# Gate and up projection: five weight pairs by seven products in eight chunks, two subtractions per chunk on GpSimd, results turned one chunk later

## The chip, the core and the metric

The kernel runs on one core of one Trainium2 chip. The time is the device time of one execution in microseconds. The trace gives the work of TensorE (PE, with its weight loads as PEld), VectorE (DVE), ScalarE (ACT), GpSimd (POOL) and SyncE (SP, which here only issues DMAs). TensorE multiplies, VectorE and ScalarE prepare the weights and finish results, GpSimd adds while it transfers (accumulating DMAs).

## The reference, cut to what matters

Two layers over 256 tokens of width 2048, all in float32:

```python
for l in range(DEPTH):                      # 2
    h = rms_norm(x, pre_mix_norm[l])
    m = hybrid_mixer(h, l, w_in[l], w_o[l], ...)      # two kinds of attention
    x = x + rms_norm(m, post_mix_norm[l])
    h = rms_norm(x, pre_ffn_norm[l])
    f = (silu(h @ w_gate[l]) * (h @ w_up[l])) @ w_down[l]   # inner width 5632
    x = x + rms_norm(f, post_ffn_norm[l])
```

The change is in the gate and up projection, `h @ w_gate` and `h @ w_up`, and in what was done ahead of time for it in the output projection of the mixer.

## The kernel before

**Precision.** A float32 weight tile is split in two parts that TensorE multiplies at full rate: `hi`, the rounded value (ScalarE, L351), and `lo`, the rest, `raw - hi` (VectorE, L354; called a rest below). The activations are split in the same way, once. A product of float32 quality is three matmuls of 512 columns (`product`, L1113): high by `hi`, high by `lo`, low by `hi`.

**Chunks and pairs.** The inner width 5632 is cut into 11 chunks of 512 columns, c = 0 to 10. The sum over 2048 inputs is cut into 8 pairs `kp` of twice 128 rows. A weight tile is 128 x 1024: two K blocks of one pair and chunk. Per chunk, four PSUM banks hold gate and up for two groups of 128 tokens.

**Eight or seven.** A pair done plainly (`eight`) takes 2 K blocks x 2 token groups x 2 matrices = 8 products, 24 matmuls. Some pairs (`seven`, `seven_products`) use a scheme of seven products (21 matmuls) that treats gate and up of one pair as a 2 x 2 block matrix. It needs sums of weight tiles: T, the up tile with the gate tile's first half added by an accumulating DMA on GpSimd's queue (L298); then on VectorE the second half of T (L334), and G, the gate tile plus that (L335); each sum is split into high and low like a weight (L319 on ScalarE, L320 on VectorE: `hi`/`lo` of T, `Th`/`Tl` of the half and of G). It also needs sums of activations, made once per layer and pair by `pair_sums`, at places in the table `FORM_AT` of (chunk, place in the chunk): pair. Four more banks collect p1, p6, p7 and q5; at the end of the last seven of a chunk, `shared_part` (L1157 on ScalarE, L1158 to L1161 on VectorE) folds them into four tiles `w`, which are added to the chunk's four banks when these are done.

Which pairs go by seven is given by `gate_sevens` (L70): c=0 has two, c=1 three, most chunks four (pairs 2, 4, 5, 6), and the chunks in `MORE_AT`, 7 and 9, five (2 to 6). For these two chunks the sums of pairs 3 and 5 are made ahead of time by `foresee` (L244), while the output projection runs, stored to DRAM, and loaded back in `summed` (L281) as T, a third tile and W.

**Results.** At the end of a chunk VectorE adds `w` to the banks (L1308, L1310), ScalarE takes Silu (L1309), VectorE multiplies (L1311). `flip` then turns the result with four transposes per token group on TensorE (L1317) and a copy on ScalarE (L1318); it starts 7 ticks after the chunk's end, so in the middle of the next chunk's first pairs, each group at a tick of its own.

**Order.** The code calls engines in program order; a scheduler of the framework places instructions of different engines, and each engine, and each DMA queue, then works through its own list in order. The weights come in one stream in the order of use (`weight_order`, L77), with `LOOKAHEAD` four tiles split ahead. Buffers: `raw` 4, `hi` and `lo` 6 each, G 3, T 4. `not_ahead`, `behind` and `after_rests` keep some loads and VectorE instructions behind named others; `put_away` stores parts of x at the chunks in `AWAY_AT`.

Of the kernel before, what the change touches and what calls it, by code (L numbers as in the profile page):

```python
# [9 lines left out]
F32 = mybir.dt.float32  # L10
# [48 lines left out]
AWAY_AT = (3, 4, 5, 6)  # L59
# [6 lines left out]

FORESEEN_PER_LAYER = [(c, kp) for c in FORESEEN for kp in FORESEEN[c]]


def gate_sevens(c):  # L70

    if c in MORE_AT:
        return MORE_SEVEN
    return (FIRST_SEVEN, NEXT_SEVEN)[c] if c < 2 else SEVEN


def weight_order():  # L77
# [9 lines left out]
    for l in range(L):  # L87
# [14 lines left out]
        for c in range(FF // CW):  # L102
            for kp in FIRST_ORDER if c == 0 else range(KT // 2):
# [60 lines left out]
def kernel(  # L164
# [37 lines left out]

    ready = {}
# [3 lines left out]
    def fetch(upto):  # L207
        while len(raws) < min(upto, len(stream)):
            i = len(raws)
            for j in range(i, min(i + EARLY + 1, mix_raw[3])):  # L210
                if j in sevens and j not in sums and not (j in foreseen and j > i + 1):
# [30 lines left out]
    foreseen, found, thirds = {}, {}, []  # L242

    def foresee(l):  # L244

        jobs = [plan[l]["up"][c, kp] for c, kp in FORESEEN_PER_LAYER]
        tiles = {}

        def summed_up(i):
            g, u = tiles[i]  # L250
            k = kept.tile([P, 4, CW], F32, name=f"foreseen{i}")
            with after_rests():
                sums_in_place(g, u, True)
            nc.gpsimd.dma_start(k[:, 0:2, :], u)
            nc.gpsimd.dma_start(k[:, 2:4, :], g)
            foreseen[i] = k

        for n, i in enumerate(jobs):
            tiles[i] = [x_pool[0].tile([P, 2, CW], F32, tag="W", bufs=2 * len(jobs), name=f"{q}{i}") for q in ("Gf", "Tf")]
            for t, j in zip(tiles[i], (i - 1, i)):  # L260
                with in_turn():
                    nc.sync.dma_start(t, stream[j])
                yield AHEAD_PACE
            if n:
                summed_up(jobs[n - 1])
            yield AHEAD_PACE
        yield AHEAD_PACE
        summed_up(jobs[-1])

    def sums_in_place(g, u, first):  # L270

        t2 = u[:, 1, :]
        if first:
            nc.vector.tensor_tensor(out=u[:, 0, :], in0=g[:, 0, :], in1=u[:, 0, :], op=ALU.add)
        nc.vector.tensor_tensor(out=t2, in0=t2, in1=u[:, 0, :], op=ALU.subtract)
        nc.vector.tensor_tensor(out=g, in0=g, in1=t2.unsqueeze(1).to_broadcast([P, 2, CW]), op=ALU.add)

    def summed(i):

        if i in foreseen:  # L280
            kept_sums = foreseen[i]  # L281
            n = len(found)
            if n % len(FORESEEN_PER_LAYER) == 0:
                thirds.append(late_room([P, 2, CW], f"second{i}"))
            second = thirds[-1][:, n % 2, :]
            two = [mix_raw[0].tile([P, 2, CW], F32, tag="T", bufs=mix_raw[2], name=f"{q}{i}") for q in ("T", "W")]
            with not_ahead(i):
# [1196 lines left out]
```

## Time and profile before

| | |
|---|---|
| time, median of 3 runs | 2189.97 us (2189.87 to 2190.26) |
| span of the profiled execution | 2189.2 us |
| TensorE busy | 2174.7 us, 99% of the span |
| VectorE busy | 1921.7 us, 88% |
| ScalarE busy | 1378.0 us, 63% |
| GpSimd busy | 144.2 us, 7% |
| DMA | 489.30 MB, 224 GB/s on the mean |

The profile page gives the busy time of each engine, the chain of work that ended last, and groups of like instructions with their mean duration. Windows give the busy time of each engine in a stretch of the span, with the number of instructions; the timeline gives single instructions with start and duration. A matmul's row shows its length in the pipeline; what it costs is the distance between two starts. The gate and up projection of the first layer lies between about 397 and 862 us, that of the second between about 1486 and 1951 us.

### The profile page before, as it was taken

The page shows a single profiled execution, that of the slowest core. Times are in us where ns is not written, and L with a number is a line of the kernel's source. Part 1 is how long each engine was busy: PE and PEld are TensorE (multiplying, and loading weights), DVE is VectorE, ACT ScalarE, POOL GpSimd, SP SyncE. Part 2 cuts the span into 40 slices and gives each one's busy share as a digit, 9 for nine tenths or more (in the row PEclk, how much of TensorE's full clock was granted, in tenths as well). Part 3 has the DMA queues.
Part 4 walks back from the last instruction along what each step waited for, and adds up shares of the span by engine and source line. Part 5 has one row for each costly group of instructions (what it writes and reads, how often), then busy time and mean ns, then how long its engine had stood idle before and what let it go on. Part 6 is the DMA issues. An engine that isn't in the chain of part 4 may idle for free.

```text
span 2189.2 us, 28686 instructions
## 1 busy us (share of the span) xinstructions
PE 2174.7 (99%) x9980; PEld 1787.4 (82%) x9980; DVE 1921.7 (88%) x2647; ACT 1378.0 (63%) x2063; POOL 144.2 (7%) x199
## 2 busy tenths in 40 slices
PE   9999999999999999999999999999999999999998
PEld 7888888788888888888878888887788888888886
DVE  7888659999999999989878886699999999999997
ACT  7666665756656666666665656657566566666664
POOL 1100000010010000000010000000000100000000
PEclk9999999999999999999999999999999999999999
DMA  9545577587687786767465555775866877867673
GB/s 322 194 164 173 192 243 267 184 274 234 206 282 235 229 273 210 245 210 257 146 240 173 183 173 183 256 258 195 269 214 226 274 241 232 263 213 234 207 264 101
DMA packets 146033, 489.30 MB, mean 224 GB/s; under 512 B 16592, under 2 KB 17616, under 8 KB 145376
## 3 DMA queue, kind: packets, MB, share of 16 engines
q1 hardware_dynamic: 127712, 450.72, 58.9%
q0 software_dynamic: 17600, 36.22, 8.3%
q8 instruction: 78, 1.28, 0.2%
q10 hardware_dynamic: 576, 0.54, 0.1%
q14 instruction: 67, 0.55, 0.1%
HBM read 470.63 MB, written 16.78 MB: 223 GB/s over the span
## 4 chain that ended last, share of the span: by engine, by line
PE 92%; DVE 5%; ACT 1%; issue 1%; DMA 1%; DVEq 0%; ACTq 0%
PE c L1117 9%; PE c L1118 9%; PE c L1116 9%; PE in L1116 7%; PE in L1118 7%; PE in L1117 7%; PE dn L1368 4%; PE dn L1366 4%; PE dn L1365 4%; PE p L1117 2%; PE p L1118 2%; PE p L1116 2%; PE o L601 2%; PE o L603 2%; PE o L602 2%; DVE lo L354 1%
## 5 line engine op out<-in xcount | busy, mean ns | idle before, releaser
L354 DVE TENSOR_TENSOR lo<-raw,hi 128x1024 fp32r<-128x1024 f32 x514 | 615.2, 1219 | 90.7 <-ACT hi L351 89.8
L351 ACT ACTIVATE hi<-raw 128x1024 fp32r<-128x1024 f32 x514 | 531.3, 1055 | 183.1 <-DMA raw<-in_weights_in_turn_dram 51.3
L1116 PE MATMUL c<-hi,xF 128*128 128x512 f32 x806 | 317.2, 394 | 0.1
L1117 PE MATMUL c<-lo,xF 128*128 128x512 f32 x806 | 314.4, 390 | 1.2 <-DVE lo L354 1.0
L1118 PE MATMUL c<-hi,xF 128*128 128x512 f32 x806 | 314.0, 390 | 0.0
L1117 PEld LDWEIGHTS c<-lo,xF 128*128 128x128 f32 x806 | 151.5, 188 | 33.2 <-DVE lo L354 3.3
L1118 PEld LDWEIGHTS c<-hi,xF 128*128 128x128 f32 x806 | 151.3, 188 | 32.0 <-DVE xF L525 0.4
L1116 PEld LDWEIGHTS c<-hi,xF 128*128 128x128 f32 x806 | 151.4, 188 | 30.3 <-ACT xF L520 0.5
L298 POOL DMA_DIRECT2D T<-in_weights_in_turn_dram x106 | 92.2, 869 | 1257.8 <-DMA T<-in_weights_in_turn_dram 434.6
L1365 PE MATMUL dn<-hi,jh 128*128 128x512 f32 x432 | 168.2, 389 | 0.0
L1366 PE MATMUL dn<-lo,jh 128*128 128x512 f32 x432 | 168.1, 389 | 0.0
L354 DVE TENSOR_TENSOR lo<-G,hi 128x1024 fp32r<-128x1024 f32 x114 | 138.8, 1218 | 21.1 <-ACT hi L351 21.0
L319 ACT ACTIVATE hi<-T 128x1024 fp32r<-128x1024 f32 x114 | 119.7, 1050 | 41.9 <-PE c L1118 23.9
L320 DVE TENSOR_TENSOR lo<-T,hi 128x1024 fp32r<-128x1024 f32 x114 | 138.8, 1217 | 3.2 <-ACT hi L319 2.3
L351 ACT ACTIVATE hi<-G 128x1024 fp32r<-128x1024 f32 x114 | 120.0, 1053 | 30.1 <-PE c L1118 17.4
L319 ACT ACTIVATE Th<-G 128x1024 fp32r<-128x1024 f32 x106 | 111.8, 1055 | 36.8 <-DVE G L335 35.3
L320 DVE TENSOR_TENSOR Tl<-G,Th 128x1024 fp32r<-128x1024 f32 x106 | 129.1, 1218 | 5.5 <-ACT Th L319 5.3
L1368 PE MATMUL dn<-hi,jl 128*128 128x512 f32 x432 | 133.0, 390 | 0.0
L1116 PE MATMUL in<-hi,xT 128*128 128x512 f32 x328 | 131.0, 401 | 1.1 <-ACT hi L921 1.1
L1116 PE MATMUL in<-hi,xI 128*128 128x512 f32 x328 | 131.2, 401 | 0.0
L335 DVE TENSOR_TENSOR G<-G,T 128x1024 f32<-128x1024 f32 x106 | 129.3, 1220 | 1.7
L1117 PE MATMUL in<-lo,xI 128*128 128x512 f32 x328 | 128.1, 390 | 0.3 <-DVE lo L354 0.3
(485 smaller groups left out, 4786.7 us busy)
## 6 DMA issues: line engine op xcount, KB each, us to landing
raw<-in_weights_in_turn_dram SPq DMA_DIRECT2D x514, 512.0 KB, 4.7
G<-in_weights_in_turn_dram SPq DMA_DIRECT2D x114, 512.0 KB, 5.8
T<-in_weights_in_turn_dram SPq DMA_DIRECT2D x106, 512.0 KB, 6.4
T<-in_weights_in_turn_dram POOLq DMA_DIRECT2D x106, 256.0 KB, 7.2
GU<-in_weights_in_turn_dram SPq DMA_DIRECT2D x32, 512.0 KB, 6.5
Gf<-in_weights_in_turn_dram SPq DMA_DIRECT2D x8, 512.0 KB, 6.0
Tf<-in_weights_in_turn_dram SPq DMA_DIRECT2D x8, 512.0 KB, 6.7
V<-in_weights_in_turn_dram SPq DMA_DIRECT2D x8, 512.0 KB, 5.2
```

Of the source, the lines that this page charges most:

```text
L298: nc.gpsimd.dma_start(sums[i][:, 0, :], stream[i - 1][:, 0, :], accum_op=ALU.add)
L319: nc.scalar.activation(h, w, AF.Copy)
L320: nc.vector.tensor_tensor(out=l, in0=w, in1=h.bitcast(F32), op=ALU.subtract)
L335: nc.vector.tensor_tensor(out=g, in0=g, in1=t2.unsqueeze(1).to_broadcast([P, 2, CW]), op=ALU.add)
L351: nc.scalar.activation(hi, raw, AF.Copy)
L354: rest = nc.vector.tensor_tensor(out=lo, in0=raw, in1=hi.bitcast(F32), op=ALU.subtract)
L1116: nc.tensor.matmul(a, sh, hi, start=first, stop=False, skip_group_check=open_sums[0])
L1117: nc.tensor.matmul(a, sh, lo, start=False, stop=False, skip_group_check=open_sums[0])
L1118: nc.tensor.matmul(a, sl, hi, start=False, stop=last, skip_group_check=open_sums[0])
L1365: nc.tensor.matmul(accs[c, t], sh, hi[:, kk, :], start=first, stop=False, skip_group_check=open_sums[0])
L1366: nc.tensor.matmul(accs[c, t], sh, lo[:, kk, :], start=False, stop=False, skip_group_check=open_sums[0])
L1368: nc.tensor.matmul(accs[c, t], sl, hi[:, kk, :], start=False, stop=last, skip_group_check=open_sums[0])
```

## The change

Chunks c = 2 to 9 (the third to the tenth) now all have five pairs by seven products, 2 to 6, in the order of pairs 0, 2, 1, 3, 4, 5, 6, 7, so that a plain pair stands between the first and the second of them; c=10 keeps four. Nothing is done ahead of time in the output projection any more.

In c = 2 to 10, the rests of the gate tiles of the second and third pair of the chunk are subtracted by GpSimd in place of VectorE. The first of them waits, by an added dependency, for the last matmul of the newest seven-product pair that stands in the program, that is, of the chunk before.

The result of a chunk stays in PSUM a step longer: the up part is added in place in its bank, and the last multiplication reads the bank and writes the result into a part of the room that the next chunk's turned result will take. It is turned in the next chunk's last pair, both groups of transposes together.

A plain pair of gate and up issues its 24 matmuls in another order: per K block and token group, low by `hi` for gate and up, then high by `hi` for both, then high by `lo` for both. `pair_sums(3)` moves from c=4 to c=1, and the four stores of x from c = 3, 4, 5, 6 to 1, 3, 4, 5.

```diff
 NEXT_SEVEN = (4, 5, 6)
 MORE_SEVEN = (2, 3, 4, 5, 6)
-MORE_AT = (7, 9)
-FORESEEN = {7: (3, 5), 9: (3, 5)}
-AHEAD_AT = 8
-AHEAD_PACE = 2
-FORM_AT = {(0, 1): 4, (0, 2): 6, (0, 5): 5, (1, 3): 2, (4, 3): 3}
+MORE_AT = (2, 3, 4, 5, 6, 7, 8, 9)
+MORE_ORDER = (0, 2, 1, 3, 4, 5, 6, 7)
+FORM_AT = {(0, 1): 4, (0, 2): 6, (0, 5): 5, (1, 3): 2, (1, 5): 3}
...
+AFTER = mybir.DependencyInfo(mybir.DependencyClass.Sync, mybir.DependencyReason.DATA)
...
-AWAY_AT = (3, 4, 5, 6)
+AWAY_AT = (1, 3, 4, 5)
...
+def gate_order(c):
+
+    if c in MORE_AT:
+        return MORE_ORDER
+    return FIRST_ORDER if c == 0 else tuple(range(KT // 2))
...
+    helped = {}
+    for lay in plan:
+        for c in range(2, FF // CW):
+            for n in (1, 2):
+                helped[lay["gate"][c, gate_order(c)[n]]] = n == 1
+    newest_seven = [None]
...
-    def foresee(l):
...
-        if i in foreseen:
-            kept_sums = foreseen[i]
...
-                loads.append(nc.sync.dma_start(two[0][:, 0, :], kept_sums[:, 0, :]))
-                loads.append(nc.sync.dma_start(two[0][:, 1, :], stream[i][:, 1, :]))
-                loads.append(nc.sync.dma_start(second, kept_sums[:, 1, :]))
-                loads.append(nc.sync.dma_start(two[1], kept_sums[:, 2:4, :]))
...
             lo = wpool.tile([P, 2, CW], F32R, tag="lo", bufs=6, name=f"lo{i}")
+            if i in helped:
+                rest = nc.gpsimd.tensor_tensor(out=lo, in0=raw, in1=hi.bitcast(F32), op=ALU.subtract)
+                if helped[i]:
+                    tc.add_manual_dep(rest.ins, newest_seven[0].ins.name, AFTER, reason="the shared port")
+                ready[i] = (hi, lo)
+                fed[0] += 1
+                continue
             with behind():
...
         for n, job in enumerate(todo):
             if n % 2 == 0:
                 tick()
-            product(*job)
+            newest_seven[0] = product(*job)
...
-        new_x_pool(f"ahead{l}")
-        start(foresee(l), AHEAD_AT)
...
+        def turned(c):
+
+            for t in range(NT):
+                pb = (acc_bank if c % 2 else bank)(f"actT_ps{l}_{c}_{t}")
+                for j in range(4):
+                    nc.tensor.transpose(pb[:, j * P : (j + 1) * P], results[c][t][:, j * P : (j + 1) * P], ident)
+                nc.scalar.copy(act[c][:, :, t * P : (t + 1) * P], pb.rearrange("p (k q) -> p k q", k=4))
+            yield
...
-                    for col, (hi, lo) in enumerate((g, u)):
-                        product(banks[2 * t + col], stat, (hi[:, kk, :], lo[:, kk, :]), first and kk == 0, last and kk == 1)
+                    two = banks[2 * t : 2 * t + 2]
+                    for part, j, n in ((1, 0, 0), (0, 0, 1), (0, 1, 2)):
+                        for a, w in zip(two, (g, u)):
+                            nc.tensor.matmul(a, stat[part], w[j][:, kk, :], start=first and kk + n == 0, stop=last and kk == 1 and n == 2)
...
+                if c and n == 7:
+                    start(turned(c - 1), 4)
...
-            sg = [w[0], w[2]]
-            for t, u in ((0, w[1]), (1, w[3])):
-                nc.vector.tensor_tensor(out=sg[t], in0=banks[2 * t], in1=sg[t], op=shared_sign(t, 0))
-                nc.scalar.activation(sg[t], sg[t], AF.Silu, scale=rs[t][:, 0:1])
-                nc.vector.tensor_tensor(out=u, in0=banks[2 * t + 1], in1=u, op=ALU.add)
-                nc.vector.scalar_tensor_tensor(out=sg[t], in0=u, scalar=rs[t][:, 0:1], in1=sg[t], op0=ALU.mult, op1=ALU.mult)
+            for t in range(NT):
+                nc.vector.tensor_tensor(out=w[2 * t], in0=banks[2 * t], in1=w[2 * t], op=shared_sign(t, 0))
+                nc.scalar.activation(w[2 * t], w[2 * t], AF.Silu, scale=rs[t][:, 0:1])
+            for t in range(NT):
+                nc.vector.tensor_tensor(out=banks[2 * t + 1], in0=banks[2 * t + 1], in1=w[2 * t + 1], op=ALU.add)
+            for t in range(NT):
+                nc.vector.scalar_tensor_tensor(
+                    out=results[c][t], in0=banks[2 * t + 1], scalar=rs[t][:, 0:1], in1=w[2 * t], op0=ALU.mult, op1=ALU.mult
+                )
+        start(turned(LAST), DEFER_ACT)
```

More of the change, by code (lines that the diff above doesn't have):

```diff
@@ L102, in weight_order @@
         for c in range(FF // CW):
-            for kp in FIRST_ORDER if c == 0 else range(KT // 2):
+            for kp in gate_order(c):
                 lay["gate"][c, kp] = queue_pair("w_gate", l, kp, c)
@@ L210, in fetch @@
             for j in range(i, min(i + EARLY + 1, mix_raw[3])):
-                if j in sevens and j not in sums and not (j in foreseen and j > i + 1):
+                if j in sevens and j not in sums:
                     summed(j)
@@ L1276 @@
             mine = gate_sevens(c)
-            order = FIRST_ORDER if c == 0 else tuple(range(KT // 2))
+            order = gate_order(c)
             if c == 0:
```

74 lines of the change are left out of this document (15 added, 59 removed).

## The prediction

> **What bounds the kernel now.** I read the page first (its busy table and the chain that ended last), then the windows of single gate/up chunks, then the timeline inside them, and the rows of GpSimd last.
>
> ```profile
> span 2189.2 us, 28686 instructions
> PE 2174.7 (99%) x9980; PEld 1787.4 (82%) x9980; DVE 1921.7 (88%) x2647; ACT 1378.0 (63%) x2063; POOL 144.2 (7%) x199
> PE 92%; DVE 5%; ACT 1%; issue 1%; DMA 1%; DVEq 0%; ACTq 0%
> ```
>
> TensorE is busy 99% of the span and holds 92% of the chain, so the time is a count of matmuls times a pitch, plus the few places where VectorE holds it up. The windows show that VectorE stands close behind (chunk numbers c are the code's, from 0):
>
> ```profile
> core 0: us, PE busy (x) PEld busy (x) DVE busy (x) ACT busy (x) POOL busy (x), PEclk, DMA share, GB/s
> 300.00:377.60 77.60, 77.60 (x375) 65.03 (x374) 64.99 (x98) 46.31 (x96) 4.34 (x8) 1.00 0.74 263
> 439.70:485.40 45.70, 45.06 (x201) 36.46 (x200) 43.80 (x59) 27.30 (x32) 4.37 (x5) 1.00 0.81 263
> 568.00:611.00 43.00, 42.87 (x193) 35.20 (x192) 40.85 (x50) 26.20 (x31) 3.49 (x4) 1.00 0.70 217
> 651.90:693.60 41.70, 41.70 (x189) 34.55 (x189) 38.96 (x43) 25.38 (x30) 3.48 (x4) 1.00 0.78 248
> 693.60:734.70 41.10, 41.10 (x187) 34.03 (x186) 38.99 (x43) 26.78 (x32) 3.47 (x4) 1.00 0.77 253
> ```
>
> The rows are the end of the output projection, c=1, c=4, c=6 (four K pairs by seven products) and c=7 (five, two of them with sums made ahead). Clock 1.00 throughout. In c=6 and c=7 TensorE never pauses; VectorE idles only 2.7 us of 41.7 and 2.1 us of 41.1. In c=1 and c=4 TensorE pauses 0.6 and 0.1 us; the chain passes there through VectorE's splits of a sum (Tl), once behind `pair_sums(2)`, once behind `pair_sums(3)`:
>
> ```profile
> 470.30 0.60 DVE T L334
> 470.90 1.14 DVE lo L354
> 472.04 1.15 DVE Tl L320
> 473.23 0.50 PE p L1117
> ...
> 602.65 1.23 DVE Tl L320
> 603.92 0.50 PE p L1117
> ```
>
> TensorE's pitch and the price of a turn of a result (four transposes) stand in the timeline of c=6:
>
> ```profile
> 659.87 0.39 PE L1116 MATMUL c<-hi,xF 128*128 128x512 f32 x1
> 660.10 0.39 PE L1117 MATMUL c<-lo,xF 128*128 128x512 f32 x1
> 660.33 0.40 PE L1118 MATMUL c<-hi,xF 128*128 128x512 f32 x1
> 660.56 0.60 PE L1317 MATMUL actT_ps<-ident,w 128*128 128x128 f32 x4
> 660.92 0.48 PE L1116 MATMUL c<-hi,xF 128*128 128x512 f32 x1
> 661.23 0.39 PE L1117 MATMUL c<-lo,xF 128*128 128x512 f32 x1
> ```
>
> Starts lie 0.227 us apart (660.33 less 659.87, halved, within rounding); a group of four transposes takes 0.36 us, and the matmul behind it 0.31 instead of 0.23.
>
> **The change part by part.** *Fewer matmuls.* Pairs by seven per layer go from 43 (2, 3, seven chunks of 4, two of 5) to 49 (2, 3, eight of 5, one of 4): 12 more, each 21 matmuls for 24, so 36 x 0.227 = 8.2 us less. Both groups of transposes of a chunk now stand together: one slow matmul less (0.08 us) in 20 chunks, 1.6 us. On TensorE alone: -9.8 us. A chunk of five then needs the 41.1 us of the c=7 row less 0.1.
>
> *VectorE's load.* Its prices:
>
> ```profile
> 687.59 0.69 DVE L1158 TENSOR_TENSOR w<-p,w 128x512 f32<-128x512 f32 x1 [0.64 <-PE p L1118]
> 688.31 0.69 DVE L1159 TENSOR_TENSOR w<-p,w 128x512 f32<-128x512 f32 x1
> 689.04 0.69 DVE L1160 TENSOR_TENSOR w<-q,w 128x512 f32<-128x512 f32 x1
> 689.65 0.68 DVE L1161 TENSOR_TENSOR w<-q,w 128x512 f32<-128x512 f32 x1
> 690.24 2.35 DVE L354 TENSOR_TENSOR lo<-raw,hi 128x1024 fp32r<-128x1024 f32 x2
> 692.51 0.68 DVE L1308 TENSOR_TENSOR w<-c,w 128x512 f32<-128x512 f32 x1
> 693.11 0.68 DVE L1310 TENSOR_TENSOR w<-c,w 128x512 f32<-128x512 f32 x1
> 694.31 0.74 DVE L1311 SCALAR_TENSOR_TENSOR w<-w,rs_ffn,w 128x512 f32<-128x512 f32 x1
> 694.97 0.68 DVE L1310 TENSOR_TENSOR w<-c,w 128x512 f32<-128x512 f32 x1
> ```
>
> From start to start: wide 1.14 (690.24 to 692.51 for two), half 0.60, L1311 0.66, and 0.72 where one waits for the one before. A chunk of four has 24 wide, 8 half and ten result instructions (6.1): 27.4 + 4.8 + 6.1 = 38.3, against 38.96 in its row, so 0.7 for such waits. A chunk of five after the change: 16 rests less 2 that go to GpSimd, and per seven G's sum and that sum's split (14 + 10 = 24 wide), 10 half, ten results: 27.4 + 6.0 + 6.1 + 0.7 = 40.2 us of 41.0. VectorE's slack shrinks from 2.1 or 2.7 to 0.8 us per chunk, in eight chunks in a row, and that is before GpSimd gets in its way.
>
> *Two rests on GpSimd.* The trace has no such instruction of 1024 columns; the nearest are the rotations:
>
> ```profile
> L874 POOL TENSOR_TENSOR ra<-tok,rope_sb x16: 458/466/1539, 48.6 to 1235.7; 128x128 f32<-128x128 f32 x16
> L875 POOL TENSOR_TENSOR rb<-tok,rope_sb x16: 312/322/1363, 49.0 to 1237.0; 128x64 f32<-128x64 f32 x16
> ...
> 56.08 0.46 POOL L874 TENSOR_TENSOR ra<-tok,rope_sb 128x128 f32<-128x128 f32 x1
> 56.12 1.50 DVE L320 TENSOR_TENSOR lo<-GU,hi 128x1024 fp32r<-128x1024 f32 x1 [1.13 <-ACT hi L319]
> 56.50 1.30 POOL L875 TENSOR_TENSOR rb<-tok,rope_sb 128x64 f32<-128x64 f32 x1
> ...
> 1184.67 1.37 DVE L1000 TENSOR_TENSOR w<-in,w 128x512 f32<-128x512 f32 x2 [0.49 <-PE in L1118]
> 1184.71 0.32 POOL L875 TENSOR_TENSOR rb<-tok,rope_sb 128x64 f32<-128x64 f32 x1
> ```
>
> Medians 466 ns at 128 columns and 322 at 64 give 2.25 ns a column, so 466 + 896 x 2.25 = 2.5 us at 1024 (an estimate). The two engines exclude each other where both read two SBUF tiles: L320, 1.23 in the chain above, took 1.50 behind a GpSimd start, and L875, 0.32 alone, took 1.30 behind L320. With one input in PSUM (L1000) both run at full speed. The largest delay of VectorE that these rows show is 0.27 us, since the GpSimd instruction was so short; the other end is the whole 2.5. I take the whole, as L320's delay ends about where L874's 0.46 does. With 0.27 a rest the stalls below would nearly vanish, and the sum would be the second rival's. The Trainium skill ("SBUF — State Buffer", Who interferes with whom) says that the one that comes second is blocked for the whole instruction, which speaks against the change; by it the sum is the one below.
>
> So what VectorE has in its queue while each rest runs decides. Let T be the end of a chunk's last seven-product matmul. Rest one waits for T (the added dependency) and runs to T+2.6. At c=5 to c=9 VectorE's queue has its four shared-part instructions, all with a PSUM input, from T-1.3 (the sum it needs ends six matmuls before T) to T+1.4; the next wide one waits until T+2.5. Rest two waits for the split on ScalarE, which the queue there puts behind the first Silu: T+8.8 to T+11.2, while VectorE runs the last PSUM instructions. Counting the queue on from T+2.5 with the pitches above, the last result is out at T+11.1, and the split of n=5's sum (n is the place in the chunk), the tightest, at T+32.5; TensorE needs it 5 x 4.8 us and one eight later, at T+33.7. Margin 1.2 us, loss 0: VectorE's block falls into its own wait. The results now hold their PSUM banks until that T+11.1; the next chunk's first seven wants the last of them at T+13.1, 2.0 us later.
>
> At the three boundaries before, the queues stand otherwise. c=1 to 2: ScalarE has two raw splits, which wait for the end of the chunk's last pair (T+5.9), ahead of the G split that VectorE's next wide instruction needs; it comes 3.0 us later than in the steady boundary, 1.8 beyond the margin (the PSUM bank comes 1.0 late, inside the 1.8). c=2 to 3: one wide instruction stands inside the shared part, 1.6 late, 0.4 beyond. c=3 to 4: rest two runs T+7.0 to T+9.5 in front of a wide one, 1.9 late, 0.7 beyond; c=4 to 5 carries 0.2 of it on. Sum 3.1 us per layer, between 0 (margins hold) and 7 (no margin).
>
> *The rest.* `pair_sums(3)` moves from c=4 to c=1, before the last sum's split: two instructions of 256 columns stand ahead of it, some 0.35 us each by the 0.60 of 512: +0.7 per layer. c=4 gets back its pause, -0.4 (0.13 in row 568.00, and 603.92's 0.50 for 0.23). The sums ahead of time leave the output projection, where TensorE's row is 77.60 of 77.60: 0, hidden by matmuls either way; if their loads had cost anything it is within 0.5. Of DMAs, 16 loads and stores per layer go from the projection, and the 16 that fetch the sums back from the chunks; ten accumulating ones per layer come on GpSimd's queue:
>
> ```profile
> L298 POOL DMA_DIRECT2D T<-in_weights_in_turn_dram x106 | 92.2, 869 | 1257.8 <-DMA T<-in_weights_in_turn_dram 434.6 <-DVE w L1161 123.4 <-DVE Tl L320 115.2
> G<-in_weights_in_turn_dram SPq DMA_DIRECT2D x4, 512.0 KB, 4.3
> ...
> L351 ACT ACTIVATE hi<-raw 128x1024 fp32r<-128x1024 f32 x514 | 531.3, 1055 | 183.1 <-DMA raw<-in_weights_in_turn_dram 51.3 <-PE c L1118 36.4 <-issue 35.3
> ```
>
> GpSimd then works 5 x 0.87 + 2 x 2.5 = 9.3 us of a chunk. Behind rest one's wait for T stands the accumulation for n=5, needed only 25 us later; SP's raw loads behind rest two are due 30 us later. G has three buffers: n=6's load can go only after n=3's sums are split, T+20.3; 4.3 and a split of 1.06 (rows above) bring it to T+25.9, and VectorE comes to it at T+26.2. Cost 0, with 0.3 us in hand. The earlier put-away is one more transfer in c=1, whose DMA share is 0.81: 0 to 0.5. Low parts used last in an eight relax its deadline by four matmuls, 0.9 us, where nothing waits: 0.
>
> Sum: -9.8 + 2 x (3.1 + 0.7 - 0.4) = -3.0 us. The profiled execution has a span of 2189.2 and the median of the runs is 2189.97, 0.8 around it, which I keep: 2187.0 us.
>
> **The rivals.** *Slower: GpSimd's block makes VectorE the bound in every chunk.* Place: the second rest of each chunk, if its split comes early on ScalarE and it meets a wide instruction. Price: 1.1 + 1.7 us blocked, less 0.8 slack, 2.0 us in 16 chunks, 32 - 9.8: 2212; with half of the chunks hit, 2197 to 2202. It decides once a steady chunk blocks VectorE more than 0.8 us beyond its own wait for the shared part. For it: L320's 1.50. Against it: the queue's order at c=5 to 9.
>
> *Faster, with no stall at all.* The early boundaries' delays stay within margins, since VectorE starts a chunk ahead, or blocks are shorter than the instruction: -9.8 + 0.6 gives 2180.8. For it: c=7 ran with 39.0 of 41.1 and no pause.
>
> *The load of G is the new wait.* If it lands after 6 us and not 4.3, VectorE waits 1.4 us in each of 16 chunks, 0.6 beyond slack: +9.6, 2196.6. Against it: few loads are in flight then.
>
> **How the numbers follow.** Within 0.2%, 4.4 us, is about what a measurement of this kernel can tell from no change. My forecast, 2182 to 2191, has 0.40, split by 2185.6 nearly in halves; no stall 0.23; block in every chunk 0.27; load of G 0.10. Faster 0.41, same 0.25, slower 0.34. The range leaves out 1 in 10 at each side: from 2179.5 (no stall and the put-away and projection free) to 2204 (most chunks blocked).
>
> **What would show it.** TensorE 36 matmuls of 512 columns fewer; windows of c=5, 6 and 8 at 41.0 us with TensorE unbroken, c=2 to 4 longer than 41.0 with waits for Tl or for a bank; GpSimd rests of 2.5 us, and VectorE's wide instructions of over 2 us beside rest one. Wrong if steady chunks are longer than 41.3, if rests last over 3 us, or if waits for G's load appear at ScalarE's splits.

## The result and the profile after

The changed kernel takes 2204.06 us (2203.53 to 2204.40, five runs) where the kernel before, run beside it, takes 2189.97: a ratio of 1.0064, 95% interval 1.0052 to 1.0076. It is slower by some 14 us; 2187.0 was predicted. The profiled execution has a span of 2202.3 us, 13.1 more than before.

The page of the changed kernel: span, busy time of each engine, and the chain that ended last.

```profile
span 2202.3 us, 28747 instructions
PE 2175.5 (99%) x9944; PEld 1782.5 (81%) x9944; DVE 1947.0 (88%) x2651; ACT 1397.5 (63%) x2087; POOL 245.7 (11%) x239
PE 84%; DVE 10%; DMA 2%; issue 2%; ACT 1%; DVEq 0%; SPq 0%; ACTq 0%
```

TensorE has the 36 matmuls fewer that were predicted (9944 for 9980), but its share of the chain has fallen from 92% to 84% and VectorE's has doubled. To see where, I cut the first layer's gate and up projection at the start of each chunk's first VectorE instruction of the shared part (L1120 after the change; called P1 below). The length of a window is then one interval from chunk to chunk. Windows of the changed kernel, c=0 to 1, 1 to 2, 2 to 3, 3 to 4, then the steady c=5 to 6 and 7 to 8:

```profile
core 0: us, PE busy (x) PEld busy (x) DVE busy (x) ACT busy (x) POOL busy (x), PEclk, DMA share, GB/s
439.14:481.95 42.81, 42.31 (x186) 34.41 (x185) 41.23 (x60) 26.55 (x30) 7.52 (x7) 1.00 0.92 294
481.95:525.72 43.77, 41.83 (x181) 32.40 (x180) 43.30 (x46) 26.77 (x31) 10.59 (x8) 1.00 0.69 206
525.72:569.15 43.43, 41.17 (x182) 32.88 (x181) 42.90 (x46) 26.56 (x31) 9.15 (x7) 1.00 0.81 238
569.15:611.55 42.40, 41.18 (x185) 33.62 (x184) 42.33 (x45) 26.66 (x32) 9.21 (x7) 1.00 0.78 239
653.53:694.33 40.80, 40.80 (x186) 33.80 (x185) 40.36 (x45) 26.61 (x32) 9.13 (x7) 1.00 0.83 240
736.17:776.98 40.81, 40.81 (x186) 33.83 (x185) 40.35 (x45) 26.68 (x32) 9.23 (x7) 1.00 0.81 240
```

The steady chunks run nearly as predicted: 40.8 us with TensorE unbroken in these two, 41.0 to 41.8 in their neighbours (in the longest, c=6 to 7, TensorE pauses 0.2 us). The early ones are 42.4 to 43.8 us long, and from c=1 on VectorE is busy for all but half a microsecond of each. The timeline of VectorE, GpSimd and TensorE at c=1 to 2, where it begins:

```profile
479.68 2.36 DVE L316 TENSOR_TENSOR lo<-raw,hi 128x1024 fp32r<-128x1024 f32 x2
481.95 0.69 DVE L1120 TENSOR_TENSOR w<-p,w 128x512 f32<-128x512 f32 x1
482.55 2.81 DVE L280 TENSOR_TENSOR lo<-T,hi 128x1024 fp32r<-128x1024 f32 x1
485.29 0.68 DVE L1121 TENSOR_TENSOR w<-p,w 128x512 f32<-128x512 f32 x1
...
488.82 2.89 DVE L280 TENSOR_TENSOR Tl<-T,Th 128x512 fp32r<-128x512 f32 x1
...
479.62 4.67 POOL L309 TENSOR_TENSOR lo<-G,hi 128x1024 fp32r<-128x1024 f32 x1 [3.88 <-ACT ss L1095]
488.33 2.83 POOL L309 TENSOR_TENSOR lo<-raw,hi 128x1024 fp32r<-128x1024 f32 x1 [0.35 <-ACT hi L306]
...
479.08 0.39 PE L1080 MATMUL c<-Th,xF 128*128 128x512 f32 x1
479.31 1.07 PE L1244 MATMUL c<-hi,xF 128*128 128x512 f32 x4
```

The last matmul of the chunk's last seven is the one at 479.08, and GpSimd's rest one, tied to it, begins at 479.62. But VectorE is late: it still makes two of its own rests and comes to P1 only at 481.95. So rest one stands beside wide instructions. It is held up itself (4.67 us), then holds up the split of T, 2.81 us for 1.22; rest two does the same to a half-width split, 2.89 us for 0.69. That is 3.8 us of VectorE at this boundary. Two facts make it: VectorE's lateness, and the split of T, which stands inside the shared part in VectorE's list at c=1 to c=4. At c=4 the second alone is enough: P1 is half a microsecond ahead of rest one, as at c=5, and the split of T still takes 2.68 us:

```profile
611.55 0.68 DVE L1120 TENSOR_TENSOR w<-p,w 128x512 f32<-128x512 f32 x1
612.88 2.68 DVE L280 TENSOR_TENSOR lo<-T,hi 128x1024 fp32r<-128x1024 f32 x1
...
612.08 2.40 POOL L309 TENSOR_TENSOR lo<-G,hi 128x1024 fp32r<-128x1024 f32 x1 [4.20 <-PE c L1080]
```

What VectorE's instructions take beyond 1.22 us (wide) or 0.69 us (half) adds up to 3.8, 3.4, 2.8 and 2.2 us at c=1 to c=4 of the first layer (3.8, 3.1, 2.8 and 2.2 in the second). That is 12.2 us, where work of 4 x 2 x 1.14 = 9.1 us had been handed over. At c=5 to c=8 it is 0.3 to 0.8 us each. The same boundary at c=6, same kernel and views:

```profile
694.33 0.68 DVE L1120 TENSOR_TENSOR w<-p,w 128x512 f32<-128x512 f32 x1
695.05 0.69 DVE L1121 TENSOR_TENSOR w<-p,w 128x512 f32<-128x512 f32 x1
695.77 0.69 DVE L1122 TENSOR_TENSOR w<-q,w 128x512 f32<-128x512 f32 x1
696.38 0.68 DVE L1123 TENSOR_TENSOR w<-q,w 128x512 f32<-128x512 f32 x1
696.98 1.63 DVE L280 TENSOR_TENSOR lo<-T,hi 128x1024 fp32r<-128x1024 f32 x1
...
706.05 1.36 DVE L316 TENSOR_TENSOR lo<-raw,hi 128x1024 fp32r<-128x1024 f32 x1
...
695.11 2.41 POOL L309 TENSOR_TENSOR lo<-G,hi 128x1024 fp32r<-128x1024 f32 x1 [4.93 <-PE c L1080]
703.93 2.40 POOL L309 TENSOR_TENSOR lo<-raw,hi 128x1024 fp32r<-128x1024 f32 x1 [1.59 <-ACT hi L306]
```

Here P1 comes at the end of the seven, the four instructions with an input in PSUM stand together beside rest one, and both rests cost VectorE 0.4 and 0.15 us. The prediction's picture was right for this boundary. What it had too small was the loss at the early ones.

### The profile page after: what moved, and what is told of

Its sections match the earlier page's. It is cut to its first block, busy times and chain, and to the rows that moved or that the text cites. A ratio compares the mean times of both kernels' runs of the same rounds, so it can differ in the third digit from the quotient of the medians.

```text
span 2202.3 us, 28747 instructions
## 1 busy us (share of the span) xinstructions
PE 2175.5 (99%) x9944; PEld 1782.5 (81%) x9944; DVE 1947.0 (88%) x2651; ACT 1397.5 (63%) x2087; POOL 245.7 (11%) x239
## 4 chain that ended last, share of the span: by engine, by line
PE 84%; DVE 10%; DMA 2%; issue 2%; ACT 1%; DVEq 0%; SPq 0%; ACTq 0%
PE c L1244 15%; PE in L1078 7%; PE in L1080 7%; PE in L1079 7%; PE dn L1340 4%; PE dn L1341 4%; PE dn L1343 4%; PE p L1079 2%; PE p L1080 2%; PE c L1079 2%; PE c L1080 2%; PE c L1078 2%; PE o L563 2%; PE p L1078 2%; PE o L564 2%
## 5 line engine op out<-in xcount | busy, mean ns | idle before, releaser
L316 DVE TENSOR_TENSOR lo<-raw,hi 128x1024 fp32r<-128x1024 f32 x472 | 568.4, 1227 | 99.2 <-ACT hi L306 97.9
L306 ACT ACTIVATE hi<-raw 128x1024 fp32r<-128x1024 f32 x490 | 505.5, 1054 | 108.7 <-DMA raw<-in_weights_in_turn_dram 37.6
L1244 PE MATMUL c<-hi,xF 128*128 128x512 f32 x1248 | 338.5, 392 | 0.9 <-ACT act L1224 0.5
L1244 PEld LDWEIGHTS c<-hi,xF 128*128 128x128 f32 x1248 | 231.8, 188 | 50.5 <-DVE w L1121 1.3
L1244 PE MATMUL c<-lo,xF 128*128 128x512 f32 x624 | 193.4, 390 | 2.5 <-DVE lo L316 2.5
L279 ACT ACTIVATE Th<-T 128x512 fp32r<-128x512 f32 x126 | 79.0, 627 | 167.3 <-DVE T L289 149.6
L280 DVE TENSOR_TENSOR lo<-T,hi 128x1024 fp32r<-128x1024 f32 x126 | 172.4, 1368 | 2.9 <-ACT hi L279 2.8
L280 DVE TENSOR_TENSOR Tl<-G,Th 128x1024 fp32r<-128x1024 f32 x126 | 158.8, 1260 | 4.2 <-ACT Th L279 4.2
L1244 PEld LDWEIGHTS c<-lo,xF 128*128 128x128 f32 x624 | 117.1, 188 | 27.6 <-DVE lo L316 3.0
L1078 PE MATMUL in<-hi,xT 128*128 128x512 f32 x328 | 131.8, 404 | 0.6 <-ACT hi L883 0.6
L1080 PE MATMUL in<-hi,xT 128*128 128x512 f32 x328 | 128.3, 392 | 0.0
```

Source lines behind the costliest of these rows:

```text
L279: nc.scalar.activation(h, w, AF.Copy)
L280: nc.vector.tensor_tensor(out=l, in0=w, in1=h.bitcast(F32), op=ALU.subtract)
L306: nc.scalar.activation(hi, raw, AF.Copy)
L316: rest = nc.vector.tensor_tensor(out=lo, in0=raw, in1=hi.bitcast(F32), op=ALU.subtract)
L1078: nc.tensor.matmul(a, sh, hi, start=first, stop=False, skip_group_check=open_sums[0])
L1080: return nc.tensor.matmul(a, sl, hi, start=False, stop=last, skip_group_check=open_sums[0])
```

## The experiments

Two theories. *Block:* GpSimd's rests take time from VectorE at the early boundaries, because its list stands otherwise there. *Load:* five sums a chunk behind the sums of pairs in c=0 and c=1 are too much for VectorE, whatever GpSimd does. A third, *results*, was that the longer hold of the PSUM banks costs something in every chunk. Each run was compared with the kernel before on the same chip.

The intervals of the first layer by which the runs are read (us, between starts of P1; the kernels are named below):

| c to c | before | changed | rests on VectorE | fours | sums alone | fenced | one rest | six fives |
|---|---|---|---|---|---|---|---|---|
| 0-1 | 40.99 | 42.81 | 43.32 | 40.73 | 43.14 | 43.32 | 43.20 | 40.64 |
| 1-2 | 40.80 | 43.77 | 42.37 | 40.09 | 39.01 | 40.79 | 41.38 | 41.30 |
| 2-3 | 41.77 | 43.43 | 43.35 | 41.71 | 40.96 | 41.79 | 41.21 | 40.77 |
| 3-4 | 42.98 | 42.40 | 43.24 | 41.72 | 41.72 | 42.66 | 41.44 | 42.51 |
| 4-5 | 40.94 | 41.97 | 42.96 | 41.69 | 41.69 | 41.25 | 41.45 | 41.13 |
| 5-6 | 41.73 | 40.80 | 43.35 | 41.71 | 41.71 | 41.29 | 42.75 | 40.92 |
| 6-7 | 41.09 | 41.84 | 42.91 | 41.72 | 41.72 | 41.37 | 43.47 | 40.92 |
| 7-8 | 41.73 | 40.81 | 42.70 | 41.69 | 41.69 | 40.92 | 43.01 | 41.14 |

### Both rests on VectorE

```diff
-        for c in range(2, FF // CW):
+        for c in ():
             for n in (1, 2):
```

> The changed kernel, with both rests of each chunk on VectorE and none on GpSimd. My theory now (block): at the early boundaries (c=1 to c=5) GpSimd's rests stand beside wide instructions of VectorE, and each block of 1 to 2 us is time that VectorE does not have. Then the early intervals between shared parts (42.4 to 43.8 us in the changed kernel's first layer) fall to VectorE's own work, about 40.2 + 2 x 1.14 = 42.5 us or less, and the steady ones (40.8 to 41.8) rise to the same 42.5, as the rests come back: 2205 to 2217 us in all. Rival (load): five sums a chunk and the sums of pairs in c=0 and c=1 are simply too much for VectorE, and GpSimd's two rests only helped. Then the early intervals grow too, by up to 2.3 us each, to 44 to 46, and the time is 2218 to 2235.

2208.09 us against 2189.27 (ratio 1.0083, 1.0068 to 1.0098). In the first layer all intervals are alike up to c=9, 42.4 to 43.4. Windows of this kernel, c=1 to 2, 2 to 3 and 5 to 6:

```profile
481.68:524.05 42.37, 42.36 (x192) 34.50 (x191) 41.92 (x48) 26.14 (x31) 4.35 (x5) 1.00 0.74 219
524.05:567.40 43.35, 42.85 (x192) 34.42 (x191) 41.92 (x48) 26.98 (x32) 4.35 (x5) 1.00 0.80 233
653.60:696.95 43.35, 42.76 (x189) 33.38 (x187) 41.96 (x47) 26.18 (x31) 4.35 (x5) 1.00 0.75 224
```

A chunk now takes some 42.9 us, and VectorE is busy for 41.9 of them; most of the rest it waits for splits on ScalarE. Against that the early intervals of the changed kernel (43.8, 43.4, 42.4) show little gain from GpSimd's rests or none, though each pair takes 2 x 1.14 us off VectorE, while the late ones gain 2 us. At the early boundaries the block eats what the rests give; but GpSimd's help is needed too. The time lies in block's range, but not all early intervals fell to the 42.5 that block gave, and without GpSimd every chunk is too much for VectorE, as load says. Neither theory is enough.

### GpSimd's rests from c=6 on

```diff
-        for c in range(2, FF // CW):
+        for c in range(6, FF // CW):
```

> The changed kernel, with GpSimd making the two rests from c=6 on only; before that VectorE makes them. Block: the early intervals fall to 42.5 or less while the late ones stay at 41.0, so 2194 to 2201 us. Load: the early intervals grow by up to 2.3 us each, and c=6 to c=9 must work off what is behind, so 2208 to 2220 us.

2219.11 us (ratio 1.0137, 1.0122 to 1.0152): slower than with no rest on GpSimd at all, 11 us more than the run above. Block's expectation missed; the time lies in load's range, though not for its reason. Up to c=5 the intervals are those of the run above (42.3 to 43.3 in the first layer), and they grow where GpSimd sets in, to 44.25 and 43.6 us:

```profile
651.87:696.13 44.26, 40.85 (x178) 32.49 (x176) 42.78 (x46) 25.70 (x30) 10.07 (x8) 1.00 0.75 223
696.13:739.72 43.59, 41.35 (x183) 32.85 (x182) 43.59 (x46) 26.45 (x31) 9.15 (x7) 1.00 0.75 220
```

So it is not the place in the layer that makes the rests harmful. At c=5 to c=8 the split of T stands inside the shared part here too, and the rests take 3.1 to 4.2 us of VectorE at each. At c=7 P1 starts at 739.72, 0.9 us ahead of rest one, and the rests still meet T and G:

```profile
742.05 2.29 DVE L289 TENSOR_TENSOR T<-T 128x512 f32<-128x512 f32 x1
...
740.65 3.14 POOL L309 TENSOR_TENSOR lo<-G,hi 128x1024 fp32r<-128x1024 f32 x1 [6.16 <-PE c L1080]
```

There it is not lateness but what stands in VectorE's list. Why the scheduler's list is so here, no run shows.

### Fives at c=6 to c=9 only, and fours throughout

```diff
-MORE_AT = (2, 3, 4, 5, 6, 7, 8, 9)
-FORM_AT = {(0, 1): 4, (0, 2): 6, (0, 5): 5, (1, 3): 2, (1, 5): 3}
+MORE_AT = (6, 7, 8, 9)                                               # fours: ()
+FORM_AT = {(0, 1): 4, (0, 2): 6, (0, 5): 5, (1, 3): 2, (4, 3): 3}    # fours: without the last
-        for c in range(2, FF // CW):
+        for c in range(6, FF // CW):                                 # fours: ()
```

> Chunks with five seven-products are c=6 to c=9 only (before: c=7 and c=9 with sums made ahead; changed: c=2 to c=9), GpSimd's rests from c=6 on, the sums of pair 3 back at c=4. There are 24 matmuls of 512 columns more than in the changed kernel, 24 x 0.227 = 5.4 us, so 4.4 us less than before on TensorE alone. Block and load both say that the steady boundaries cost nothing: 2185 to 2189 us. A third theory (results): the results' longer hold on PSUM and the turn a chunk behind cost something in every chunk of the layer; then 2190 to 2196, with pauses of TensorE behind the act instructions in the chunks of four too.

> Only the form of the chunks is left of the change: results kept in PSUM and turned a chunk behind, an eight's low parts last, the earlier put-away; four seven-products in every chunk from c=2 on, no sums of pair 3, no rest on GpSimd. 41 pairs by seven per layer for 43 before: 12 matmuls more, +2.7 us, and 1.6 less for the transposes: 2191.1 us if this form costs nothing (block, load). If the results' hold on the banks costs (results), pauses behind act show at every boundary, and 2193 to 2200 us.

Fives at c=6 to 9: 2190.68 us (1.0005, 0.9996 to 1.0015), above what block and load said and at the lower end of what the third theory said, though not for its reason. The loss is one interval in each layer, c=5 to 6 (43.57 us in the first), where rest one came 3.9 us behind P1 and a half-width difference beside it took 3.29 us for 0.69. Fours: 2191.93 us (1.0013, 1.0004 to 1.0023); its span of 2189.9 is 0.7 above that of before and its median 2.7, where 1.1 was worked out. Its intervals are the 41.7 of a chunk of four before the change. The new form of the results costs nothing in any of them; *results* falls. It saves next to nothing either: 1.6 us less for the transposes were part of the 1.1, but the chunk of four takes 41.71 us for 41.73 before. TensorE's rows with both groups of transposes together:

```profile
649.25 1.04 PE L1223 MATMUL actT_ps<-ident,act 128*128 128x128 f32 x8
650.05 1.17 PE L1244 MATMUL c<-hi,xF 128*128 128x512 f32 x4
```

The eight take 0.80 us from start to start, more than the twice 0.36 of the two groups before, so little is left of the 0.08 us for one slow matmul less. Without that term 2.7 would have been worked out.

The fours also give a measure: less 3 x 0.227 = 0.68 us where a five stands in the interval, their intervals are what TensorE needs. Against that the changed kernel loses 2.1, 4.4, 2.4, 1.4 and 1.0 us from c=0 to c=5 in the first layer, 1.7, 5.7, 2.6, 1.4 and 1.0 in the second, 11.2 and 12.3 in all, and nothing on balance later.

### The shared part together, and the rests fenced

```diff
+                    held_sum[:] = held                       # the last instruction of the shared part
...
-        split(hi, lo, u)
+        nc.scalar.activation(hi, u, AF.Copy)
+        with tc.issue_after(held_sum[0].ins) if held_sum[1] else nullcontext():
+            nc.vector.tensor_tensor(out=lo, in0=u, in1=hi.bitcast(F32), op=ALU.subtract)
+        held_sum[1] = 0
```

and, in the fenced one, rest one waits for P1 instead of for the last seven, rest two for the split of G:

```diff
-                if helped[i]:
-                    tc.add_manual_dep(rest.ins, newest_seven[0].ins.name, AFTER, reason="the shared port")
+                tc.add_manual_dep(rest.ins, (newest_seven if helped[i] else newest_split)[0].ins.name, AFTER, reason="the shared port")
...
-            newest_seven[0] = product(*job)
+            product(*job)
...
-        nc.vector.tensor_tensor(out=w[1], in0=p6, in1=w[0], op=ALU.subtract)
+        newest_seven[0] = nc.vector.tensor_tensor(out=w[1], in0=p6, in1=w[0], op=ALU.subtract)
...
-        split(th[:, 0:2, :], tl[:, 0:2, :], g)
+        newest_split[0] = split(th[:, 0:2, :], tl[:, 0:2, :], g)
```

> The changed kernel, with one thing in VectorE's order: the split of the next chunk's first sum (lo of T) is held behind the last of the four instructions of the shared part, so that at c=1 to c=4 those four stand together, as they do by themselves from c=5 on. GpSimd's rests are as they were. Block: rest one then falls beside instructions with an input in PSUM at the early boundaries too; what it takes from VectorE there falls from 1.5 to 1.9 us to 0.3 to 0.6 us, four boundaries per layer, so some 9 us less: 2193 to 2199 us. Load: VectorE has the same work, so nothing changes: 2202 to 2206 us.

> As the run with the shared part together, and GpSimd's rests wait for VectorE: rest one for the end of the first instruction of the shared part, rest two for the end of the split of the first sum's other half (Tl of G), behind which two to four instructions with an input in PSUM stand. Same work on every engine as in the changed kernel. Block: both rests are hidden at the early boundaries, what they take from VectorE falls from 2.3 to 3.8 us a boundary to about 1.2 us, and the early intervals come to 41.0 to 42.0 us: 2186 to 2194 us. Load: the early intervals stay at 42.4 us and more: 2200 to 2207 us.

Together: 2198.10 us (1.0038, 1.0023 to 1.0053). Fenced: 2197.15 us (1.0030, 1.0018 to 1.0042). Block's figure for the first; between the theories for the second. The fenced kernel at c=1 to 2, VectorE and GpSimd:

```profile
481.69 0.68 DVE L1122 TENSOR_TENSOR w<-p,w 128x512 f32<-128x512 f32 x1
...
484.90 1.22 DVE L287 TENSOR_TENSOR lo<-T,hi 128x1024 fp32r<-128x1024 f32 x1
...
482.52 2.40 POOL L312 TENSOR_TENSOR lo<-G,hi 128x1024 fp32r<-128x1024 f32 x1 [7.11 <-issue]
```

P1 (here L1122) is just as late, 481.69 for 481.95, but rest one now waits for it, and the split of T takes 1.22 us, not 2.81. The interval falls from 43.8 to 40.8. At c=1 to c=4 of the first layer the rests take 1.2, 1.7, 2.5 and 1.2 us of VectorE, 6.4 in place of 12.2. So with the same work on every engine, order and waits alone are worth some 7 us: the block is real. Most of it comes with the order: that alone gives 6 us, and the two runs can't be told apart. But 43.3 us at c=0 to 1 is untouched, and what is left is still 16 us above the 2181 that the fours would give with 48 matmuls fewer (2191.9 - 48 x 0.227).

### One rest, and fives from c=6 on, fenced

```diff
-            for n in (1, 2):
+            for n in (1,):          # one rest
```

> As the run with both rests fenced, but rest two is VectorE's again. VectorE's work by the sum of the prediction is 40.2 + 1.14 + 0.35 (what rest one still takes) = 41.7 us a chunk, against 41.0 on TensorE. Block: all intervals from c=2 on near 41.7 to 42.0 us, early ones no longer than late ones: 2190 to 2198 us. Load: early ones 43 us and over, 2203 to 2212 us.

> The kernel with five seven-products at c=6 to c=9 only, and both rests fenced. In that kernel without the fences rest one came 3.9 us behind the start of the shared part at c=5 and the half-width difference of T beside it took 3.29 us for 0.69; the interval was 43.6 us for 41.0. Block: this interval falls to 41.0 to 41.5 us and the kernel comes to 4.4 us below before, 2184 to 2187 us, the fastest of all. If the loss at c=5 to c=6 lies in the step from four to five itself (load), it stays at 2190 to 2191 us.

One rest: 2200.64 us (1.0050, 1.0035 to 1.0065), above block's range and below load's. It became the clearest sight of the block, since one kernel shows both: in the first layer its intervals are 41.2 to 41.5 us from c=1 to c=5 and 42.7 to 43.6 behind that, up to c=9, with the same instructions in each chunk. VectorE and GpSimd at c=3 and at c=6:

```profile
564.17 0.69 DVE L1122 TENSOR_TENSOR w<-p,w 128x512 f32<-128x512 f32 x1
567.70 1.22 DVE L287 TENSOR_TENSOR lo<-T,hi 128x1024 fp32r<-128x1024 f32 x1
...
565.00 2.39 POOL L312 TENSOR_TENSOR lo<-G,hi 128x1024 fp32r<-128x1024 f32 x1 [5.48 <-issue]
...
689.81 0.68 DVE L1122 TENSOR_TENSOR w<-p,w 128x512 f32<-128x512 f32 x1
694.72 3.44 DVE L292 TENSOR_TENSOR T<-T 128x512 f32<-128x512 f32 x1
...
694.31 0.88 POOL L258 DMA_DIRECT2D T<-in_weights_in_turn_dram  x1 [8.26 <-DVE lo L287]
694.87 2.74 POOL L312 TENSOR_TENSOR lo<-G,hi 128x1024 fp32r<-128x1024 f32 x1
```

At c=3 rest one runs beside the shared part and nothing is longer. At c=6 an accumulating DMA stands ahead of it on GpSimd's queue and is issued at 694.31, when VectorE's split of a T is done; rest one follows at 694.87, 5.1 us behind P1, and the difference of T takes 3.44 us.

Fives from c=6 on, fenced: 2191.29 us (1.0007, 0.9997 to 1.0016), no better than without fences. Block's expectation missed: a fence can hold a rest back but not bring it forward, and at c=5 to 6 the accumulating DMA ahead of it had it late again (3.5 us behind P1, interval 43.1), though VectorE was on time there: P1 had waited 0.6 us for TensorE.

### The sums of pair 3 alone

```diff
-FORM_AT = {(0, 1): 4, (0, 2): 6, (0, 5): 5, (1, 3): 2}
+FORM_AT = {(0, 1): 4, (0, 2): 6, (0, 5): 5, (1, 3): 2, (1, 5): 3}     # in the kernel with fours
```

> The kernel with four seven-products in every chunk and no rest on GpSimd (2191.9 us), with one thing added: the sums of pair 3 are made in c=1 as in the changed kernel, though no seven-product uses them. It measures their price alone. By the prediction's term 0.7 us a layer: 2193.3 us, the interval from c=0 to c=1 41.4 us for 40.7. By the intervals of the changed kernel (42.8 there) 2 us or more a layer while VectorE has no slack there: 2195 to 2198 us.

2193.15 us (1.0016, 1.0007 to 1.0024). That is 1.2 above the fours by the medians and 0.7 by the ratios, whose intervals overlap; the profiled runs give 0.6 us in the first layer and nothing in the second. So the price alone is about the prediction's 0.7 us a layer or less. The windows show how, c=0 to 1, 1 to 2 and 2 to 3 of the first layer:

```profile
438.14:481.28 43.14, 42.44 (x186) 34.38 (x185) 41.23 (x61) 25.15 (x29) 3.46 (x4) 1.00 0.69 231
481.28:520.29 39.01, 39.01 (x177) 32.00 (x176) 38.45 (x44) 25.38 (x30) 3.45 (x4) 1.00 0.80 265
520.29:561.25 40.96, 40.96 (x187) 34.00 (x186) 39.05 (x44) 25.08 (x29) 3.49 (x4) 1.00 0.77 253
```

P1 at c=1 comes 2.4 us later than in the fours, and the next two chunks of four give 1.1 and 0.75 of it back. VectorE is made late by 2.4 us (a debt, as it is called below), and only 0.6 of it is left, because chunks of four follow, in which it can catch up.

### The stores of x back at c=3 to c=6

```diff
-AWAY_AT = (1, 3, 4, 5)
+AWAY_AT = (3, 4, 5, 6)      # in the fenced kernel
```

(The first of the four stores moves from c=1 to c=3, the other three by one chunk each.)

> The kernel with both rests fenced (2197.2 us), with the first put-away of x back from c=1 to c=6, as before the change. In the second layer of the changed kernel ScalarE waits 3.6 us for a load of G at c=2. If the put-away in c=1 is what delays that load, the intervals from c=0 to c=2 fall by 1 us or more a layer: 2193 to 2195.5 us. If not, it stays at 2196 to 2198 us, and the rise of the intervals at c=1 is VectorE's alone (sums of pair 3).

2224.21 us (1.0154, 1.0141 to 1.0167): neither expectation. The interval from c=1 to 2 became 55.9 us, with a wait that is in no other run; ScalarE's waits of this kernel between 470 and 660 us:

```profile
ACT ss L1097 <- DMA away_ffn<-x: 6.9, 1, 6.9
```

The split of the sums of pair 3 waits for a store of x (a put-away): they lie in room that x leaves. So the earlier store belongs to the sums in c=1, and the run says nothing on its own cost. What it was meant to test, whether that store delays a load of G, stays open: in the changed kernel ScalarE waits for a load of G at c=1 to 2 in both layers. Its waits between 482 and 526 us, and between 1574 and 1624 us:

```profile
ACT hi L306 <- DMA G<-in_weights_in_turn_dram: 2.3, 1, 2.3
...
ACT hi L306 <- DMA G<-in_weights_in_turn_dram: 3.6, 1, 3.6
```

The second layer's interval is the longer one too, 45.1 us for 43.8. The trace bounds what the load makes: what counts is VectorE's wait behind that split, 0.5 us in the first layer and 1.8 in the second, all of VectorE's idle time there. These differ by 1.3 us, as the intervals do, while the rests take 3.8 us in both. No run takes the wait away by itself.

### Fives behind a chunk of slack

```diff
-MORE_AT = (2, 3, 4, 5, 6, 7, 8, 9)
-FORM_AT = {(0, 1): 4, (0, 2): 6, (0, 5): 5, (1, 3): 2, (1, 5): 3}
+MORE_AT = (4, 5, 6, 7, 8, 9)                                          # seven fives: from 3 on
+FORM_AT = {(0, 1): 4, (0, 2): 6, (0, 5): 5, (1, 3): 2, (2, 3): 3}
-        for c in range(2, FF // CW):
-            for n in (1, 2):
+        for c in range(4, FF // CW):                                  # seven fives: 3
+            for n in (1, 2) if c > 4 else (2,):                       # seven fives: c > 3
```

with the fences; and six fives once more without them.

> Fenced rests, five seven-products at c=4 to c=9, the sums of pair 3 at c=2, and VectorE makes rest one of the first such chunk, since GpSimd's queue has it late there (c=5 to c=6 of the runs with fives from c=6 on). 24 matmuls fewer than before the change and 1.6 us for the transposes: 7.0 us less than before on TensorE. If the fence and the place of the sums settle all: 2184 to 2187 us, the fastest of all. If VectorE at 40.2 us and more of 41.0 still loses some 0.4 us in each chunk of five: 2188 to 2192 us.

> As the run with six chunks of five, but from c=3 on, right behind the chunk in which the sums of pair 3 are made. 8.4 us less than before the change on TensorE, 2181.6 us. If sums and block are separate costs, each paid once, 2185 to 2188 us. If a chunk of five has too little slack on VectorE to work off what the sums leave, the loss stays through the chunks that follow: intervals of 41.3 to 42 us to c=7, and 2190 to 2196 us.

> The kernel with five seven-products at c=4 to c=9 (2186.35 us) without the fences: VectorE's order and the waits of GpSimd's rests as in the changed kernel, all else the same. It closes the square of start (c=2 or c=4) and fences (with or without). If the block costs something wherever rests are not fenced, the split of T that stands inside the shared part at c=4 meets rest one, the intervals behind it rise by 0.5 to 1.5 us a layer: 2187.5 to 2190 us. If a chunk that starts with VectorE on time works the block off, nothing changes: 2185.5 to 2187.5 us, and the fences matter only behind a backlog.

Six fives, fenced: 2186.35 us against 2190.17 (ratio 0.9984, 0.9976 to 0.9993), faster than both kernels. Its page and the interval c=4 to 5:

```profile
span 2184.2 us, 28706 instructions
PE 92%; DVE 5%; ACT 1%; issue 1%; DMA 0%; DVEq 0%; ACTq 0%
```

```profile
603.23:644.36 41.13, 41.13 (x187) 33.98 (x186) 40.96 (x45) 26.90 (x32) 9.20 (x7) 1.00 0.83 249
```

The time lies within what was expected if fence and place of the sums settle all. TensorE is unbroken in this interval, the one to the second five, with VectorE at 40.96 of 41.13. Seven fives, the first right behind the sums: 2189.67 us (0.9999, 0.9990 to 1.0007), between its two expectations. Its matmuls should make it 1.4 us faster than six fives and it is 3.3 slower; its intervals behind the sums are 43.2, 41.5 and 41.3 us, so the debt is carried on. Six fives without fences: 2187.31 us (0.9990, 0.9981 to 0.9999), within what was expected if VectorE works the block off when it is on time (2185.5 to 2187.5). It can't be told from the fenced one, so a gain of the fences shows only where VectorE has a debt. The four corners, as ratios to before:

| | rests as changed | shared part together, rests fenced |
|---|---|---|
| fives from c=2, sums of pair 3 at c=1 | 1.0064 | 1.0030 |
| fives from c=4, sums of pair 3 at c=2 | 0.9990 | 0.9984 |

The causes are not separate. The fences, with the order of the shared part, are worth 7 us where VectorE is late and nothing that these runs resolve where it is on time; the later start is worth 10 to 16 us, though it keeps 12 matmuls, 2.7 us, that the changed kernel saves. The later start moves more than one thing: the fives, the sums of pair 3, and one rest that VectorE makes again at the first five. ScalarE's longest wait for a load of G falls with it too, from 3.6 us to 0.7. These runs don't split its worth further.

## Why the prediction was wrong

**What held.** *Fewer matmuls:* 36, and the steady chunk of five takes 41.1 us on the mean of c=5 to c=9 where 41.0 was worked out. *A rest on GpSimd:* 2.40 us when nothing is in its way, 2.5 estimated. *The block:* 0.27 us or the whole instruction were the ends; the runs show the whole (T's difference 3.44 for 0.69, so 2.75 lost beside a rest of 2.74). The Trainium skill ("SBUF — State Buffer", Who interferes with whom) says that of VectorE and GpSimd the one that comes second waits for the end of the other when VectorE's instruction has two inputs in SBUF, and that one with a single SBUF input, outside VectorE's two-port modes, isn't touched. Both agree with these rows, the second with the 0.68 to 0.69 us of the shared part beside rest one. *Steady boundaries:* almost no loss, VectorE 40.4 us busy where 40.2 was summed up, and rest one, tied to T, stands beside the shared part there, as was said. *Results and eights:* they cost 0, as the fours show; but the 1.6 us that the transposes were to save are not there, since the eight together take as long as the two groups did.

**The step that failed** is the term for the early boundaries, 1.8 + 0.4 + 0.7 + 0.2 = 3.1 us a layer and 0.7 for the sums of pair 3, so 3.8. Measured against the fours it is 11.2 and 12.3 us. Its mechanism was named, but it was sized by taking each boundary by itself, against the margin of the steady chunk, with VectorE coming to it on time and one wide instruction inside the shared part at one boundary only.
- The sums of pair 3 were priced at 0.7 as if they were time of their own. Alone they cost about that or less. What they leave is VectorE 2.4 us late at c=1, and in the changed kernel fives follow at once, with the prediction's own 0.8 us of slack; the debt is carried from chunk to chunk.
- The rests were placed from T. At c=1 to 2 P1 comes 2.3 us behind the rest that is tied to T, so rest one meets VectorE's own rests and the split of T. The rests then take 3.8 us from VectorE at that boundary, where it has 0.8 to give. At c=2 to c=4 the split of T stands inside the shared part too, and they take 3.4, 2.8 and 2.2 us, where delays of 1.6, 1.9 and none were worked out. The intervals need until c=5 to come down.
- So the loss is a debt and the blocks on top of it, carried from chunk to chunk, not a sum of four small delays, and margins of a chunk that is on time don't bound it. How much belongs to each is not shown: order and fences give back 7 of some 23 us, the later start most of it.

**The rivals.** The block in every chunk, with 2197 to 2202 us for half of the chunks hit, came nearest, with another place: not because the second rest meets a wide instruction in a steady chunk, but because at c=1 to c=4 both rests meet wide instructions, VectorE being late or the split of T standing inside the shared part. No stall at all did not happen. The load of G did become a wait in most chunks of five, and the prediction named such waits as a sign that it was wrong. They are longest at c=1 to 2, 2.3 and 3.6 us on ScalarE. But VectorE, for which 1.4 us in every chunk were put, waits 0.5 and 1.8 us there, and at most 1.0 us in any interval behind that, up to c=9 (that one is c=6 to 7 of the first layer, the 41.84 us). The range ended at 2204, just short of the time, since its upper end took the block in most chunks and no debt beside it.

## What to carry to other kernels

When an engine has 40.2 us of work in a chunk of 41.0, a cost on it is not paid where it arises: ask how much slack the chunks behind it have, and add the debt up until it is gone. Work handed to an engine that the first one excludes, as VectorE and GpSimd do here with both inputs in SBUF, helps only while it falls beside instructions that are not excluded, here those with an input in PSUM. So look at what stands in the first engine's list at that place, and tie the work to the instruction that it should run beside, not to an event on a third engine. And put one-time work (here the sums of a pair) ahead of a stretch with slack, not ahead of the tight one: two chunks less of the faster form gave the faster kernel.

## What the runs showed of the hardware

A wide subtraction on VectorE and one on GpSimd, both from SBUF, exclude each other in both directions: GpSimd's took 4.67 us for 2.40 when VectorE was at its own, VectorE's half-width one 2.89 for 0.69 when GpSimd had begun 0.5 us before it (c=1 of the changed kernel). The time spent waiting is part of the duration that the profile shows. Handing 2 x 1.14 us of VectorE's work to GpSimd then took up to 3.8 us from VectorE, a net loss (c=1 to 2), while beside instructions with an input in PSUM it took 0.5 us (c=6 of the changed kernel). An accumulating DMA ahead on GpSimd's own queue decides the same: with rest one 5.1 us behind P1, after such a DMA, it cost 2.75 us, where it had cost nothing 0.8 us behind P1 (the run with one rest, c=6 and c=3). Eight transposes of 128 x 128 together take as long on TensorE as two groups of four with matmuls between them: a chunk of four takes 41.71 us for 41.73.
